# Filling all eight input buffers at the start, and issuing nine later loads from GpSimd as 120 and 8 rows

## The chip, the cores and the metric

The kernel runs on one core of one Trainium2 chip. The metric is the device time of one execution in microseconds (us), the median over the runs named. A profile shows one execution, and its span is the time from the first to the last instruction.

## The reference

```python
# q, k: [8, 12, 1024, 64] float32
def reference(q, k):
    return np.einsum('bhid,bhjd->bhij', q, k).astype(np.float32)   # [8, 12, 1024, 1024]
```

For each of 96 heads a 1024 x 1024 score matrix is written, 4 MB in float32. The profile counts 50.33 MB read from HBM and 402.65 MB written, so outputs are eight ninths of all bytes.

## The kernel before

Heads come in 25 blocks, the first two of two heads, the others of four. A block's input comes in four pieces (two of q, two of k), each 512 KB in blocks of four heads, 4 KB in each of 128 rows. The pieces of the first three blocks go into memory that is later an output buffer ("early"), all others into a pool of eight buffers called x_sb. GpSimd casts a piece to float16, PE transposes it, VectorE copies the transposed tiles, PE multiplies, and ScalarE (5 of 8) and VectorE (3 of 8) evict the scores from PSUM into an output buffer. One DMA of 4 MB per head writes that buffer from the SyncE queue. ScalarE's queue issues the later loads.

```python
    in_pool  = ctx.enter_context(tc.tile_pool(name="in_pool", bufs=8))
    out_pool = ctx.enter_context(tc.tile_pool(name="out_pool", bufs=4))
    # ...
        def load(self, n, eng, raw=None):
            if raw is None:
                x_sb = in_pool.tile([P, self.elems], F32, tag="x")
                raw = x_sb
            self.raw[n] = raw
            start = (self.first + n // 2 * self.G) * S
            src = (qf, kf)[n % 2][start : start + self.G * S]
            pin(eng.dma_start(out=raw, in_=src.rearrange("(p r) d -> p (r d)", p=P)))
    # ... scores(): 8 x (two matmuls of 512 columns, one eviction), then
            pin(nc.sync.dma_start(out=of[self.first + n].rearrange("(p t) j -> p (t j)", p=P),
                                  in_=o_sb.rearrange("p t j -> p (t j)")))
    # ... start: blocks 0 to 2 into "early", then block 3 into four of the eight x_sb
    for n in range(4):
        blocks[3].load(n, (nc.sync, nc.scalar)[n % 2])
    # ... main loop, after each head's scores:
            b.scores(n, side)
            if i == n == 0:
                next_load()          # blocks[4:], piece by piece, nc.scalar
            next_load()
            if nxt and a == nxt.G - 1 and 0 < i + 3 < len(blocks):
                to_half(blocks[i + 3 : i + 4])      # the casts
```

## Time and profile before

The first three runs gave 1074.59 us (1074.47 to 1074.97). Runs of the same kernel fell into two groups, about 1074.3 to 1075.2 and about 1075.8 to 1076.5. The profiled execution was of the second group. What divides the groups was not studied; differences under 1.5 us below rest on several runs, not on one profile.

| what | before |
|---|---|
| time, median | 1074.59 us |
| DMA rate in the middle slices | 426 to 436 GB/s |
| busiest compute engine | PE, 69% of the span |
| first output issued | 19.56 us |

Two views need a word. In the costliest groups a line reads: source line, engine, operation, output<-input, shapes, count, then busy us and mean ns of one, then the idle time just before them and what ended most of it. In the list of DMA issues a line ends with the KB of each and the median us from issue to landing. From these two views of the kernel before:

```profile
L132 ACT COPY o_sb<-ps 128x1024 f32<-128x1024 f32 x480 | 475.9, 1013 | 554.7 <-DMA out_dram<-o_sb 347.6
...
out_dram<-o_sb SPq DMA_DIRECT2D x96, 4096.0 KB, 36.7
```

ScalarE stands idle longer than it works, and most of that waits for an output buffer to be written out. A 4 MB output needs 36.7 us, though 4 MB at 430 GB/s are 9.8 us, because three or four of them stand in the queue at once. The kernel is bound by its DMA engines.

A third reading is not printed on the page. A DMA that all sixteen engines share ends with sixteen increments of its semaphore, one per engine, and the trace records the time of each. Their spread tells how far one engine runs behind the others. I call the time from the fifteenth to the sixteenth increment **the gap**.

### The profile page before, as it was taken

The numbers are of one execution on the slowest core, as the hardware profiler recorded it, in microseconds if no ns is written. First come the engines' busy times: TensorE is split into PE (matmuls) and PEld (weight loads), VectorE is DVE, ScalarE is ACT, GpSimd is POOL, SyncE is SP. The second block draws the span as 40 slices with busy tenths as digits, with TensorE's granted clock in tenths as the row PEclk, the third lists the DMA queues.
The fourth block names the chain that finished last, engine by engine and source line by source line (L and its number), as shares of the span: only waits on it lengthen the run. The fifth ranks groups of instructions, "written<-read, shape, count | busy, mean of one in ns | idle before, by whom it ended". The sixth has DMA issues, their size and how long they took to land.

```text
span 1074.4 us, 6393 instructions
## 1 busy us (share of the span) xinstructions
PE 743.6 (69%) x2304; PEld 267.3 (25%) x2304; DVE 463.7 (43%) x384; ACT 477.2 (44%) x481; POOL 100.7 (9%) x106
## 2 busy tenths in 40 slices
PE   7977677676776757667676676767767676678740
PEld 2322222222222212222222222222222222223210
DVE  4645354452534535345353443434434444445420
ACT  4545444444444434444443544444444443544530
POOL 4100101010010100101010010100101010000000
PEclk9965555555555555555555555555555555555555
DMA  9999999999999999999999999999999999999993
GB/s 332 430 429 433 429 433 432 428 431 433 429 432 431 431 427 436 429 428 435 431 429 434 427 431 434 427 432 434 426 433 433 429 430 432 432 431 429 436 432 170
DMA packets 28257, 453.42 MB, mean 422 GB/s; under 512 B 3136, under 2 KB 3136, under 8 KB 15936
## 3 DMA queue, kind: packets, MB, share of 16 engines
q1 hardware_dynamic: 14976, 405.81, 87.7%
q10 hardware_dynamic: 13248, 47.19, 11.0%
q8 instruction: 18, 0.29, 0.1%
q14 instruction: 15, 0.12, 0.0%
HBM read 50.33 MB, written 402.65 MB: 422 GB/s over the span
## 4 chain that ended last, share of the span: by engine, by line
DMA 79%; PE 12%; ACT 4%; issue 0%; DVE 0%; ACTq 0%; POOL 0%; SPq 0%
DMA out_dram<-o_sb 79%; PE ps L128 12%; ACT o_sb L132 4%; PE t_ps L103 1%; DMA early<-in_q_dram 0%; DVE o_sb L130 0%; DVE kT L115 0%; ACTq L132 0%; POOL half_sb L88 0%; SPq L75 0%
## 5 line engine op out<-in xcount | busy, mean ns | idle before, releaser
L128 PE MATMUL ps<-kT,qT 64*128 64x512 f16 x1536 | 657.3, 621 | 289.8 <-ACT o_sb L132 286.4
L132 ACT COPY o_sb<-ps 128x1024 f32<-128x1024 f32 x480 | 475.9, 1013 | 554.7 <-DMA out_dram<-o_sb 347.6
L130 DVE COPY o_sb<-ps 128x1024 f32<-128x1024 f32 x288 | 352.7, 1225 | 568.9 <-DMA out_dram<-o_sb 404.5
L128 PEld LDWEIGHTS <-qT 64*128 64x128 f16 x1536 | 193.2, 134 | 687.0 <-issue 680.2
L88 POOL CAST half_sb<-x_sb 128x1024 f16<-128x1024 f32 x88 | 91.3, 1040 | 835.0 <-DMA x_sb<-in_k_dram 404.6
L103 PE MATMUL t_ps<-ident,half_sb 128*128 128x128 f16 x768 | 99.0, 310 | 6.1 <-POOL half_sb L88 6.1
L103 PEld LDWEIGHTS <-half_sb 128*128 128x128 f16 x768 | 74.1, 141 | 84.4 <-issue 62.4
L115 DVE COPY qT<-t_ps 128x1024 f16<-128x1024 f16 x48 | 60.6, 1263 | 7.2 <-PE t_ps L103 7.2
L115 DVE COPY kT<-t_ps 128x1024 f16<-128x1024 f16 x48 | 58.3, 1215 | 0.2 <-PE t_ps L103 0.2
L88 POOL CAST half_sb<-early 128x512 f16<-128x512 f32 (+1 forms) x12 | 8.7, 755 | 5.4 <-DMA early<-in_q_dram 5.4
L132 ACT ACT_TABLE_LOAD x1 | 1.3, 1283 | 8.8 <-DMA early<-in_q_dram 8.8
masks.py:199 POOL TENSOR_SCALAR_AFFINE_SELECT ident<-ident 128x128 f16<-128x128 f16 x1 | 0.3, 292 | 0.1
masks.py:197 POOL MEMSET ident<- 128x128 f16 x1 | 0.2, 204 | 0.3 <-POOLq L219 0.3
L219 POOL MEMSET const-float32-0.0<- 128x1 f32 x1 | 0.1, 98 | 0.2 <-issue 0.2
L219 POOL MEMSET const-bfloat16-1.0<- 128x1 bf16 x1 | 0.1, 101 | 0.0
L219 POOL MEMSET const-uint8-127<- 128x1 uint8 x1 | 0.1, 101 | 0.0
L219 POOL MEMSET const-float32-1.0<- 128x1 f32 x1 | 0.1, 98 | 0.0
## 6 DMA issues: line engine op xcount, KB each, us to landing
out_dram<-o_sb SPq DMA_DIRECT2D x96, 4096.0 KB, 36.7
x_sb<-in_k_dram ACTq DMA_DIRECT2D x44, 512.0 KB, 32.1
x_sb<-in_q_dram ACTq DMA_DIRECT2D x42, 512.0 KB, 32.1
early<-in_k_dram ACTq DMA_DIRECT2D x4, 256.0 KB, 5.0
early<-in_q_dram SPq DMA_DIRECT2D x4, 256.0 KB, 4.8
early<-in_q_dram SPq DMA_DIRECT2D x2, 512.0 KB, 7.3
early<-in_k_dram ACTq DMA_DIRECT2D x2, 512.0 KB, 7.4
x_sb<-in_q_dram SPq DMA_DIRECT2D x2, 512.0 KB, 9.3
```

Source lines behind the costliest of these rows:

```text
L88: nc.gpsimd.tensor_copy(out=self.halves[n % 2][:, :, n // 2], in_=self.raw[n].rearrange("p (r d) -> p r d", d=D),)
L103: pin(nc.tensor.transpose(t_ps[:, t], rows, ident))
L115: pin(nc.vector.tensor_copy(out=dst, in_=src))
L128: pin(nc.tensor.matmul(ps[:, js], qT[cs, g, t], kT[cs, g, js]))
L130: pin(nc.vector.tensor_copy(out=o_sb[:, t], in_=ps))
L132: pin(nc.scalar.copy(out=o_sb[:, t], in_=ps))
L219: nc = _bacc.Bacc("TRN2", target_bir_lowering=False, num_devices=1)
```

## The change

Two things are meant to fill idle DMA time at the two ends. At the start all eight x_sb buffers are loaded (blocks 3 and 4) where four were, so that the engines have work until the first output. In mid-run nine q-pieces are issued by GpSimd in two DMAs of 120 and 8 rows; at eight rows per engine, 120 rows leave one engine of sixteen free, which is meant to help an engine that lags. As eight pieces are loaded at once and one more after each head, the later loads also run two heads further ahead.

```diff
-        def load(self, n, eng, raw=None):
+        def load(self, n, eng, raw=None, parts=((0, P),)):
 ...
-            pin(eng.dma_start(out=raw, in_=src.rearrange("(p r) d -> p (r d)", p=P)))
+            src = src.rearrange("(p r) d -> p (r d)", p=P)
+            for lo, hi in parts:
+                pin(eng.dma_start(out=raw[lo:hi], in_=src[lo:hi]))
 ...
-    for n in range(4):
-        blocks[3].load(n, (nc.sync, nc.scalar)[n % 2])
+    stream = [(b, n) for b in blocks[3:] for n in range(4)]
 ...  # next_load() moves up here and takes the issuing engine and the parts
+    for n in range(8):
+        next_load((nc.sync, nc.scalar)[n % 2])
 ...
             b.scores(n, side)
-            if i == n == 0:
-                next_load()
-            next_load()
-            if nxt and a == nxt.G - 1 and 0 < i + 3 < len(blocks):
+            gp = i % 2 == 0 and n == 1 and i > 2
+            if gp:
+                next_load(nc.gpsimd, parts=((0, 120), (120, P)))
+            if nxt and a == nxt.G - 1 and i + 3 < len(blocks):
                 to_half(blocks[i + 3 : i + 4])
+            if i + n > 0 and not gp:
+                next_load(nc.scalar)
```

More of the change, by code (lines that the diff above doesn't have):

```diff
@@ L157, with next_load @@
         at += 4 * b.elems
-    for n in range(4):
-        blocks[3].load(n, (nc.sync, nc.scalar)[n % 2])
+    stream = [(b, n) for b in blocks[3:] for n in range(4)]
+    def next_load(eng, **kw):
+        if stream:
+            b, n = stream.pop(0)
+            b.load(n, eng, **kw)
+    for n in range(8):
+        next_load((nc.sync, nc.scalar)[n % 2])
     make_identity(nc, ident)
@@ L172 @@
     to_half(blocks[2:3])
-    stream = [(b, n) for b in blocks[4:] for n in range(4)]
-    def next_load():
-        if stream:
-            b, n = stream.pop(0)
-            b.load(n, nc.scalar)
     blocks[0].alloc()
```

## The prediction

> **What bounds the kernel now.** I read the page first: the busy shares, then the forty slices with the DMA row, then the queues and the chain that ended last.
>
> ```profile
> PE 743.6 (69%) x2304; PEld 267.3 (25%) x2304; DVE 463.7 (43%) x384; ACT 477.2 (44%) x481; POOL 100.7 (9%) x106
> ...
> DMA  9999999999999999999999999999999999999993
> GB/s 332 430 429 433 429 433 432 428 431 433 429 432 431 431 427 436 429 428 435 431 429 434 427 431 434 427 432 434 426 433 433 429 430 432 432 431 429 436 432 170
> ...
> q1 hardware_dynamic: 14976, 405.81, 87.7%
> q10 hardware_dynamic: 13248, 47.19, 11.0%
> ...
> DMA 79%; PE 12%; ACT 4%; issue 0%; DVE 0%; ACTq 0%; POOL 0%; SPq 0%
> ```
>
> The sixteen DMA engines are busy in every slice but the last, at 426 to 436 GB/s; no compute engine passes 69%, and 79% of the chain is output DMA. So the bytes bound it, and no byte is removed. What is to be had lies in the first slice (332 GB/s) and the last (170). I therefore asked for the windows of both ends (columns: busy time per engine, then granted clock, DMA share, GB/s).
>
> ```profile
> 16.00:18.00 2.00, 2.00 (x14) 1.04 (x13) 1.52 (x3) 0.75 (x1) 0.34 (x1) 1.00 0.93 371
> 18.00:20.00 2.00, 1.76 (x8) 0.44 (x5) 1.56 (x2) 1.47 (x2) 2.00 (x3) 1.00 0.22 35
> 20.00:22.00 2.00, 1.93 (x6) 0.60 (x5) 0.61 (x1) 1.76 (x3) 1.65 (x2) 1.00 1.05 274
> ...
> 1052.00:1056.00 4.00, 0.00 (x0) 0.00 (x0) 0.00 (x0) 0.00 (x0) 0.00 (x0) 0.50 0.95 410
> 1056.00:1060.00 4.00, 0.00 (x0) 0.00 (x0) 0.00 (x0) 0.00 (x0) 0.00 (x0) 0.50 0.42 180
> 1060.00:1062.00 2.00, 0.00 (x0) 0.00 (x0) 0.00 (x0) 0.00 (x0) 0.00 (x0) 0.50 0.08 33
> 1068.00:1070.00 2.00, 0.00 (x0) 0.00 (x0) 0.00 (x0) 0.00 (x0) 0.00 (x0) 0.50 0.08 33
> ```
>
> The tail is the find. From 1060 to 1072 us the share is about one sixteenth: **one engine of sixteen** is still writing. A transfer's end is sixteen semaphore increments, one per engine, and the trace has the time of each. For the last output the first came at 1056.23, the eighth at 1058.71, the fifteenth at 1060.51 and the sixteenth at 1072.83 us: 12.3 us for one engine alone. The same gap was 0.07 us for the output issued at 75.9, 1.06 at 163.7, 6.06 at 430.9, 8.83 at 697.5 and 11.61 at 875.2. So one engine falls behind evenly, all run long. The packets say how: of the 12288 packets of 32 KB nearly all took 1213 ns, but between 60 and 1045 us 769 took 3 to 90 ns more, 15.6 us in total, and one engine's share of 96 outputs is 96 x 8 = 768. It is slower by some 20 ns a packet (1.7%) and is never idle.
>
> Then the start, from the timeline of the first 25 us.
>
> ```profile
> 7.05 1.70 ACTq L75 DMA_DIRECT2D x_sb<-in_k_dram  x2
> 8.78 1.28 ACT L132 ACT_TABLE_LOAD   x1 [8.78 <-DMA early<-in_q_dram]
> 10.39 1.01 ACT L132 COPY o_sb<-ps 128x1024 f32<-128x1024 f32 x1 [0.33 <-PE ps L128]
> 18.53 1.01 ACT L132 COPY o_sb<-ps 128x1024 f32<-128x1024 f32 x1 [1.77 <-PE ps L128]
> 18.53 0.34 ACTq L75 DMA_DIRECT2D x_sb<-in_q_dram  x1
> 19.56 23.82 SPq L136 DMA_DIRECT2D out_dram<-o_sb  x4
> ```
>
> Inputs run dry at 18.1 us; the packets restart at 19.6 with two loads, slowly (274 GB/s at first), and the first output issues at 19.56. ACT's first copy comes only after its queue has issued its loads, the last of which waited until 8.4 us for an earlier transfer's semaphore.
>
> **What the Trainium skill says.** "DMA: Bandwidth & Descriptors", section "Where 436 GB/s comes from", puts the ceiling at sixteen ports times 27.2 GB/s, 435 GB/s; the slices at 426 to 436 agree, so the middle cannot be sped up. The same page, "Latency and other measured facts", says engines 7 and 15 are usually slower and guesses at the rings of GpSimd-issued DMAs. This trace agrees that one engine is slower, but no GpSimd-issued DMA exists in it, so the guessed cause does not hold here; the trace does not number the engine. The same page, "Why a DMA increments its semaphore by 16 and not by 1", says how many engines a DMA uses: a 128-partition copy takes all sixteen; some GpSimd-issued direct copies are given ceil(partitions/16) rows per engine, so that 100 partitions leave engine 15 without data. No run shows that yet; the change stands on it. "SBUF — State Buffer", section "SBUF: two separate sides", warns that GpSimd cannot write descriptors while a VectorE operation holds the shared port. GpSimd casts of 1040 ns with no spread beside DVE copies (43% busy) show no such lock-out here.
>
> **The change, part by part.**
>
> (a) *Nine of the 88 x_sb loads as 120 + 8 rows from GpSimd.* With 8 rows per engine, 120 rows fill engines 0 to 14 and leave the sixteenth free; 8 rows then go as one row each to eight engines. A 4 KB packet repeats every 155 ns on a busy engine. The sixteenth engine is spared 9 x 8 x 155 = 11.2 us. Eight others get 9 x 155 = 1.4 us more. The pieces are one in two blocks, about 89 us apart by the chain's 44.4 us per block; 1.24 us relieved each time against a growth of 12.3 us / 1000 us x 89 = 1.1 us: the sizes match so well that I take the sixteenth engine to be the target. Issuing costs nothing on the path: POOL is 9% busy, and its DMAs stand in its order behind casts that are long done.
>
> (b) *Four more loads at the start.* They are 2 MB, 4 x 8 x 155 = 5.0 us of every engine, so data lasts to 18.1 + 5.0 = 23.1 us instead of 18.1. But two more go through ACT's queue, and the instruction order of the changed kernel shows them ahead of the table load, each waiting for a reused semaphore: by the trace of before, those early transfers land at 11.11 and 13.67 us. ACT then loads its table at about 14.1 and first copies at 15.4 instead of 10.39. PE has three output banks and stalls on the fourth tile. Walking copies of 1.01 (ACT) and 1.22 us (DVE) and matmul pairs of 0.9 us forward in their order, I get the first output at 22.9 instead of 19.56 us. So the hole is not filled outright: loads end at 23.1 and the output's packets begin 1 to 3.7 us after issue (3.7 is what the first one of before took, 23.3 - 19.56). Loss before: 1.6 us empty plus about 1.4 us of slowed load packets (23 us excess over 16 engines). Loss after: 0.8 to 3.5 us. Net gain some 0.8 us, between -0.5 and +2. Later outputs (29.6, 38.3 us) come before the engines have drained.
>
> (c) *Loads running two heads further ahead.* The queue was never empty; worth nothing.
>
> Sum: the slow engine ends at 1072.8 - 0.8 - 11.2 = 1060.8; the fifteenth, with added rows, at 1060.5 - 0.8 + 1.4 = 1061.1. With 1.6 us from last landing to the end of the span (1074.4 - 1072.8), that is 1062.7 us. Both ends meet, so no further gain hides behind it.
>
> **The rivals.** *First: the relieved engine is another one.* Nothing numbers the slow engine. If it is among those that take the extra 8 rows, it ends 1.4 us later, some 1075 us; if the engine left out changes from one DMA to the next, the relief is spread and the slow one gets nothing net, some 1074. For it: the page's two candidates, 7 and 15. Against: the fit of nine pieces to the lag, in size and spacing. I give these together 30%. *Second: the start gets worse*, by ACT's blocked queue, as worked out in (b): up to 1.5 us against the gain. That is included. *Third: GpSimd's DMAs are costly themselves*, by slow descriptor writing or by slowing an engine whose ports hold the rings. A late piece is covered by about five heads (55 us) from issue to cast; eighteen such DMAs against 184 others can hardly slow an engine by more than 1 to 3 us. That would give 1063 to 1066. *Fourth: the slow engine had held back the others*, so that more than the tail comes back. The fifteen were busy throughout, so there is no more to give.
>
> **Range and chances.** About 65% for 1060.5 to 1064.5, about 30% for 1072.5 to 1075.5, the rest between or outside. The point leans on the first, with a little for the third rival: 1063.5. Over 2% faster means under 1053.1. The engines' own load of 96 x 8 x 1.2095 + 88 x 8 x 0.155 + about 10 us of early loads = 1048 us, the first bytes at 1.75 us, some 3 us lost before the first output, 196 semaphore writes of 9 ns (1.8), the added rows (1.4) and the end (1.6) already come to 1057.5: 2%. Slower by over 2% needs 21 us more, which no step offers: 2%.
>
> **What would show it.** Right: one-sixteenth windows after the other engines end shrink from 12 us to under 3; the gap of sixteenth to fifteenth increment stays below 3 us all run instead of growing to 12; the GpSimd-issued loads carry 120- and 8-row packets with the main queues' 4 KB packets fewer by 9 x 128; ACT's table load near 14 us, first output at 22 to 24. Wrong: the gap again grows to 11 to 14 us (another engine relieved); table load still at 8.8 (my reading of the queue fails); DMA share under 0.9 in a middle slice (a new wait).

## The result

Four runs of the changed kernel gave a median of 1075.04 us (1074.91 to 1075.21), beside 1074.78 us for four of the kernel before. The ratio is 1.000, with a 95% interval of 0.9983 to 1.0017. (A ratio here is the mean time of one kernel's runs over that of the other's of the same rounds, so it is not quite the ratio of the medians quoted.) Nothing was gained.

The page of the changed kernel, in the same rows as before: the DMA row and the GB/s of the forty slices, the queues (packets, MB, share of sixteen engines' span) and the chain.

```profile
DMA  9999999999999999999999999999999999999993
GB/s 391 425 425 433 426 432 430 421 434 429 433 420 434 434 424 431 433 429 430 430 429 428 431 432 428 430 434 427 435 432 422 434 435 427 431 431 438 430 430 171
...
q1 hardware_dynamic: 15264, 406.85, 88.2%
q10 hardware_dynamic: 11664, 41.42, 9.5%
q0 software_dynamic: 1584, 4.72, 1.1%
...
DMA 77%; PE 12%; ACT 4%; issue 0%; ACTq 0%; SPq 0%
```

The first slice rose from 332 to 391 GB/s, so the start did improve. The last slice is 171 where it was 170: the tail is as it was. The new row q0 is GpSimd's nine pieces, 4.72 MB. Its 1584 packets are 1152 of 4096 bytes, the nine times 128 rows, and 432 of four bytes.

The windows of the start (columns: busy time and count of PE, PE's weight loads, VectorE, ScalarE and GpSimd, then granted clock, DMA share, GB/s):

```profile
16.00:18.00 2.00, 2.00 (x5) 0.58 (x5) 0.96 (x1) 1.82 (x3) 0.00 (x0) 1.00 1.04 416
18.00:20.00 2.00, 2.00 (x12) 0.91 (x12) 1.39 (x2) 0.96 (x1) 0.07 (x1) 1.00 1.01 403
20.00:22.00 2.00, 1.76 (x7) 0.55 (x4) 1.56 (x3) 1.20 (x2) 2.00 (x3) 1.00 1.04 416
22.00:24.00 2.00, 2.00 (x5) 0.53 (x4) 0.89 (x1) 1.82 (x3) 1.93 (x2) 1.00 1.28 533
```

No window is empty any more. From 16 to 22 us the kernel before moved 371, 35 and 274 GB/s and this one 416, 403 and 416. The differences sum to 555 GB/s over 2 us, 1.1 MB, which is some 2.6 us at 430 GB/s (an estimate from these windows). The 533 GB/s from 22 to 24 us is no true rate: a window counts a packet whole where it starts, and the first 32 KB packets start here. The timeline of ScalarE shows the delay that the prediction walked through:

```profile
6.94 6.67 ACTq L77 DMA_DIRECT2D x_sb<-in_k_dram  x4
13.64 1.28 ACT L134 ACT_TABLE_LOAD   x1 [13.64 <-DMA early<-in_k_dram]
14.93 2.84 ACT L134 COPY o_sb<-ps 128x1024 f32<-128x1024 f32 x3
```

The table load did move behind the four issues, from 8.78 to 13.64 us, and the first copy to 14.93. The first output was issued at 21.84 us.

The windows of the tail, the same columns:

```profile
1058.00:1060.00 2.00, 0.00 (x0) 0.00 (x0) 0.00 (x0) 0.00 (x0) 0.00 (x0) 0.50 0.15 66
1060.00:1062.00 2.00, 0.00 (x0) 0.00 (x0) 0.00 (x0) 0.00 (x0) 0.00 (x0) 0.50 0.04 16
...
1068.00:1070.00 2.00, 0.00 (x0) 0.00 (x0) 0.00 (x0) 0.00 (x0) 0.00 (x0) 0.50 0.04 16
1070.00:1072.00 2.00, 0.00 (x0) 0.00 (x0) 0.00 (x0) 0.00 (x0) 0.00 (x0) 0.50 0.04 16
```

One engine of sixteen still writes alone, for over ten microseconds. The last output's increments came at 1052.84 (first), 1055.95 (8th), 1060.50 (15th) and 1071.88 us (16th). The gap is 11.4 us where it was 12.3. In the kernel before, the first and the eighth came at 1056.23 and 1058.71, about three microseconds later: some engines did end earlier, but not the one that sets the end.

**Which engine carries what.** The packets in the trace do not name their engine, but on a busy engine each packet starts 3 to 4 ns before the last one ends, so a chain of packets can be followed. In the stretches around the GpSimd pieces this yields sixteen chains: one with no 4 KB packet of the piece, seven with eight, eight with nine. That is the arithmetic of the prediction: 120 rows on fifteen engines, the 8 further rows on eight. The slow engine can be told by its 32 KB packets, which take some 21 ns longer in the median. In every piece that could be read (for instance 470 to 492 and 740 to 757 us) it carried **nine**. The change gave the lagging engine one row more, not eight fewer. Where packets of two engines end together, their chains can be mistaken for each other; the increments, read under gp128 below, do not have this weakness and say the same.

### The profile page after: what moved, and what is told of

The parts are those of the page before. It is cut to its first block, busy times and chain, and to the rows that moved or that the text cites. A ratio compares the mean times of both kernels' runs of the same rounds, so it can differ in the third digit from the quotient of the medians.

```text
span 1073.1 us, 6371 instructions
## 1 busy us (share of the span) xinstructions
PE 744.3 (69%) x2304; PEld 267.6 (25%) x2304; DVE 463.7 (43%) x384; ACT 476.9 (44%) x481; POOL 106.8 (10%) x124
## 3 DMA queue, kind: packets, MB, share of 16 engines
q0 software_dynamic: 1584, 4.72, 1.1%
## 4 chain that ended last, share of the span: by engine, by line
DMA 77%; PE 12%; ACT 4%; issue 0%; ACTq 0%; SPq 0%
DMA out_dram<-o_sb 71%; PE ps L130 11%; DMA x_sb<-in_q_dram 6%; ACT o_sb L134 4%; PE t_ps L105 0%; ACTq L134 0%; SPq L138 0%
## 5 line engine op out<-in xcount | busy, mean ns | idle before, releaser
L90 POOL CAST half_sb<-x_sb 128x1024 f16<-128x1024 f32 x88 | 88.4, 1044 | 801.7 <-PE t_ps L105 414.4
L77 POOL DMA_DIRECT2D x_sb<-in_q_dram x18 | 9.5, 532 | 0.0
```

The lines of the kernel that those rows point to most:

```text
L77: pin(eng.dma_start(out=raw[lo:hi], in_=src[lo:hi]))
L90: nc.gpsimd.tensor_copy(out=self.halves[n % 2][:, :, n // 2], in_=self.raw[n].rearrange("p (r d) -> p r d", d=D),)
```

## The experiments

All edits are to the changed kernel, unless it is said otherwise. The kernel before ran beside each call.

### start_only, gp128, gp_only: the parts alone

```diff
 # start_only: every later load from ScalarE, as before
-            gp = i % 2 == 0 and n == 1 and i > 2
+            gp = False
 # gp128: GpSimd issues the same nine pieces, each as one DMA of 128 rows
-                next_load(nc.gpsimd, parts=((0, 120), (120, P)))
+                next_load(nc.gpsimd)
 # gp_only: the kernel before, with the nine pieces from GpSimd as 120 + 8 rows
+            if i % 2 == 0 and n == 1 and i > 2:
+                next_load(nc.gpsimd, parts=((0, 120), (120, P)))
+            else:
+                next_load()
```

> The start of the change alone: eight x_sb buffers filled at the beginning, every later load from ACT as 128 rows, no GpSimd DMA. Theory (the two parts cancel: the start gains about 2 us, the uneven pieces cost the slow engine 9 rows x 155 ns = 1.4 us): 2.0 to 2.5 us faster than before, ratio 0.9977 to 0.9982. Rival 1 (the start gains nothing, as ACT's late table load eats it): within 0.5 us of before. Rival 2 (GpSimd DMAs cost as such): says nothing of this run. The gap between fifteenth and last increment of the last output stays at 11 to 13 us in all.

> The changed kernel, but the nine GpSimd loads are one DMA of 128 rows each. Theory (only the extra row on the slow engine costs): as start_only within 0.5 us, so 1.4 us faster than the changed kernel. Rival 2 (a GpSimd DMA costs whatever its shape, by descriptors or ring traffic): as the changed kernel or slower, near 1075. In the trace every engine should carry 8 data packets of each piece.

> The kernel before with nine of its later loads issued by GpSimd as 120 and 8 rows, its start untouched. Theory (slow engine gets 9 rows instead of 8 of each piece): 1.4 us slower than before, ratio 1.001 to 1.002, gap of the last increment 12 to 14 us. Rival (the spared engine is the slow one after all, and something else ate the gain): 8 to 11 us faster, gap under 4 us.

Measured, five rounds each, with 1074.79 us for the kernel before:

| kernel | median us | ratio to before (95%) |
|---|---|---|
| start_only | 1072.63 | 0.9979 (0.9967 to 0.9992) |
| gp128 | 1073.55 | 0.9989 (0.9976 to 1.0001) |
| gp_only | 1076.68 | 1.0018 (1.0004 to 1.0032) |

The start alone gains 2.2 us. Handing nine whole pieces to GpSimd gives back 0.9 us (1073.55 - 1072.63, with ranges that do not touch: 1072.29 to 1073.00 and 1073.26 to 1074.02). Cutting each into 120 + 8 gives back 1.5 us more (1075.04 - 1073.55; after_again, on the same chip as gp128, gives 1.6). Nine pieces, each with one 155 ns row and one 9 ns semaphore write more for the slow engine, come to 9 x 0.164 = 1.48 us. The sum -2.2 + 0.9 + 1.5 = +0.2 gives back the measured 0.3, as it must, since the three are steps from one kernel to the next; what supports it from outside is the 1.48. On the start of before, the second part alone makes the kernel slower, by 1.9 us, where 0.9 + 1.5 would be 2.4.

Two expected gaps were missed: gp_only's is 11.3 us (12 to 14 expected), and start_only's 4.6 us (11 to 13), with the fifteenth increment at 1064.50, the sixteenth at 1069.07 and the other fourteen by 1061.68. So in that execution two engines lag, and the gap alone understates the lag. The gap of gp128's last output is 11.0 us against 11.4 with the cut. By the increments of the slow engine, eight outputs around a piece take 88.87 us in gp128 and 89.03 in the changed kernel, a difference of 0.16 per piece: the ninth row is seen piece by piece.

### locate: which cuts hit the slow engine

Each of the nine pieces was cut in another way, to see from the slow engine's increments where the rows fall.

```diff
+    # ... cut(): the rows as ranges of these sizes
+    shapes = [cut(120, 8), cut(120, 4, 4), cut(120, 2, 2, 2, 2), cut(120, 3, 3, 2),
+              cut(120, 5, 3), cut(120, 6, 2), cut(120, 7, 1), cut(*[8] * 16), cut(P)]
-                next_load(nc.gpsimd, parts=((0, 120), (120, P)))
+                next_load(nc.gpsimd, parts=shapes.pop(0) if stream else ())
```

> Look only: the changed kernel with nine different cuts of the GpSimd pieces: 120 rows and then 8; 4+4; 2+2+2+2; 3+3+2; 5+3; 6+2; 7+1; then sixteen DMAs of 8; then one of 128. If a DMA of n < 16 rows puts one row on each of the n lowest engines, the slow engine (the one whose 32 KB packets take some 20 ns more) carries 9 rows of the first piece, and the others tell its number: 10 or 8 (4+4), 12 or 8 (2+2+2+2), and so on; 16 rows of the piece of sixteen DMAs if it is among the lower eight, 0 if not. Rival (a moving first engine): its counts follow no such pattern. The time should grow by the extra rows, 8 x 155 ns = 1.2 us for the sixteen-DMA piece, and at most 1.5 us for the rest.

1076.75 us, not a time to compare. The clear mark is the eighth piece: sixteen DMAs of 8 rows cost the slow engine 1.56 us more than the whole piece at the same place in gp128, about what eight extra rows (8 x 0.155 = 1.24) and further semaphore writes make. So the slow engine is among those that take one of 8 rows. The remainders cut as 5 + 3, 6 + 2 and 7 + 1 moved it by 0.28, 0.15 and 0.23 us, those as 3 + 3 + 2 and four times 2 by 0.07 and 0.12. These fit an engine that takes a row of a 5-row DMA and not of a 4-row one, which would be the fifth, but differences of 0.1 us are too near the scatter to rest on.

### hw120: the same cut from ScalarE's queue

```diff
-                next_load(nc.gpsimd, parts=((0, 120), (120, P)))
+                next_load(nc.scalar, parts=((0, 120), (120, P)))
```

> The changed kernel, but its nine uneven pieces (120 and 8 rows) are issued by ACT instead of GpSimd. Theory (start gain 2.2 us; GpSimd issue as such costs 0.9 us, the uneven cut 1.5 us by the slow engine's ninth row): 2.2 - 1.5 = 0.5 to 1.0 us faster than before, ratio about 0.9993. Rival (the cost is all GpSimd's): as start_only, 0.998. Rival (ACT's cut spares the slow engine): 8 us faster or more.

A miss: 1077.55 us against 1074.92, ratio 1.0019 (1.0007 to 1.0032). The GB/s row of its page shows something else than the question asked:

```profile
GB/s 388 423 425 435 423 415 429 427 433 433 425 432 434 427 429 435 427 427 437 427 428 428 424 433 423 424 433 421 394 429 431 391 419 427 434 432 431 429 430 286
```

Two slices in the middle fall to 394 and 391 GB/s: the DMA engines ran short there. The fifteenth increment of the last output came at 1067.31 and the sixteenth at 1073.23 us, so the gap shrank to 5.9 us because the other engines had become late too. The extra issues in ScalarE's queue wait for earlier landings, and the copies behind them wait along; I did not prove that this is the cause. The run says nothing about what a row or a GpSimd issue costs. That stays open.

### lower_half: nine pieces, each as sixteen DMAs of 8 rows

If the slow engine is among the eight that always take the 8 rows, it now gets sixteen rows a piece instead of eight.

```diff
-                next_load(nc.gpsimd, parts=((0, 120), (120, P)))
+                next_load(nc.gpsimd, parts=[(r, r + 8) for r in range(0, P, 8)])
```

> The changed kernel with each of the nine GpSimd pieces cut into sixteen DMAs of 8 rows, so that eight engines take 16 rows each and eight none. Theory (the slow engine is one of those eight): 9 x 7 rows x 155 ns = 9.8 us more than the changed kernel and some 2 to 3 us for the many semaphore writes, 1086 to 1089 us, gap of the last increment over 15 us. Rival (the slow engine is the one that 120 rows spare, or any of the upper eight): it loses 9 x 8 rows, 11 us, and the time is 1064 to 1068.

Measured 1088.08 us, ratio 1.0118 (1.0104 to 1.0132), as expected under the theory that the slow engine is one of those eight. The windows of its tail:

```profile
1066.00:1068.00 2.00, 0.00 (x0) 0.00 (x0) 0.00 (x0) 0.00 (x0) 0.00 (x0) 0.50 0.46 197
...
1070.00:1072.00 2.00, 0.00 (x0) 0.00 (x0) 0.00 (x0) 0.00 (x0) 0.00 (x0) 0.50 0.57 246
...
1082.00:1084.00 2.00, 0.00 (x0) 0.00 (x0) 0.00 (x0) 0.00 (x0) 0.00 (x0) 0.50 0.08 33
```

About half of the engines work from 1066 to 1072 us: those are the eight with the doubled rows (the 8th increment came at 1065.94, the 15th at 1077.68). Then one remains, to 1085.07. The slow engine is in the loaded half. The gap is 7.4 us, not over 15 as expected, because the fifteenth engine is then one of the seven others with doubled rows; from the eighth increment to the last it is 19.1 us.

### extra_mm: more PE instructions, no more data

What makes that engine slow? In the kernel before, the delay of slow 32 KB packets grows, though not at every step, with the number of matmuls and transposes that start while the packet is under way (the 769 packets delayed by 3 to 90 ns between 60 and 1045 us; a few of them are of other engines):

```
PE instructions in the packet's time     0      1      2      3      4      5      6      7
mean delay of a slow packet, ns        9.5   13.1   21.4   19.4   28.8   30.1   28.6   40.1
```

The last compute instruction ends at 1040.7 us, and the slow engine's packets at the end, from 1062.7 us on, are not delayed: each takes 1213 ns. So I added 1536 tiny matmuls, whose results the next matmul overwrites, to start_only.

```diff
 # on top of start_only
                     js = slice(j * 512, (j + 1) * 512)
+                    tiny = slice(j * 512, j * 512 + 16)
+                    pin(nc.tensor.matmul(ps[:, tiny], qT[cs, g, t], kT[cs, g, tiny]))
                     pin(nc.tensor.matmul(ps[:, js], qT[cs, g, t], kT[cs, g, js]))
```

> start_only with a matmul of 16 columns ahead of each of the 1536 score matmuls (overwritten by it; the result stays right). It asks what slows the slow engine. In the trace its delay per 32 KB packet goes with the number of PE instructions in it, some 3 to 4 ns each. Theory (instruction traffic of the core slows that engine): 1536 more matmuls and weight loads add 4 to 9 us to its lag, gap 15 to 21 us, time 4 to 8 us over start_only, with the other fifteen engines ending where they did. Rival (the delay is the engine's own): time within 0.7 us of start_only, 1072.6, gap 11 to 13 us.

Measured 1080.27 us, ratio 1.0046 (1.0032 to 1.0059), 7.6 us over the median of start_only (from another call). Not a byte of input or output was added. The slow engine's last increment came at 1077.03 where it had been 1069.07 us (8.0 later), the eighth at 1061.61 where it had been 1058.73 (2.9 later). That the others would stay as they were was wrong by 2.9 us, but the slow engine lost over twice as much. By its increments, four outputs take it 44.36 us in start_only and 44.72 in extra_mm, which is 11 ns for each of 32 packets. The expected gap of 15 to 21 us was missed (10.6, against 4.6 in start_only), since the fifteenth increment is late too, at 1066.41, 4.8 us after the eighth. The first outputs were issued at the same time in both (22.01 and 21.89 us), so the start is not the cause. The instruction fetches, from the pages of start_only and of extra_mm, did grow:

```profile
q8 instruction: 18, 0.29, 0.1%
```

```profile
q8 instruction: 30, 0.49, 0.2%
```

Twelve more fetches of 16 KB, each about 0.94 us of one engine, are 11 us, or 0.7 us if spread over sixteen. Where chains of packets could be followed, in the kernel before and in extra_mm, the fetches ran on other engines than the slowest, and that engine's own 32 KB packets were the ones prolonged. So the fetched bytes do not explain its lag. What is shown is that the lag grows when PE has more instructions; through which path is not shown. One rival was not tested: the profiler records every instruction, and every run has a span and a clock, so the traffic of that recording may itself be what delays the engine.

### locate2: other access patterns

```diff
+    shapes = [ ...  # 120 and 8 rows as column halves, as two 1 KB chunks per row ("3d"),
+               ...  # 100 + 28 rows, 60 + 60 + 8 rows, 127 rows "3d" + 1 row, 128 rows "3d" ]
-                next_load(nc.gpsimd, parts=((0, 120), (120, P)))
+                next_load(nc.gpsimd, parts=shapes.pop(0) if stream else ())
```

> Look only: other forms of the nine pieces (halves of columns, three-dimensional patterns, 100+28 rows, 60+60+8, 127+1), to see whether any of them places its rows on other engines than the lowest. If they all fill from the lowest engine, the slow engine never carries fewer rows than an even cut gives it, and 11 us cannot be had this way. If some start at a moving engine, the engine without rows differs from piece to piece.

1083.31 us, useless as a time: the piece of 127 rows in two chunks went to a single engine, landed only at 899.7 us, 159 us after it was issued, and left the other engines short of work at its end (one slice fell to 207 GB/s). What it was worth running for: with rows in two chunks, a half-piece of 120 rows left out a *different* engine each time. Two engines then carried four to five rows of a piece, the others nine. This is the other rule that the Trainium skill states in "DMA: Bandwidth & Descriptors", section "Why a DMA increments its semaphore by 16 and not by 1": the count of engines is the largest number up to 16 that divides the rows, and for GpSimd's DMAs with fewer than sixteen engines they are consecutive ones "from a round-robin cursor". The plain rows tried here filled from the lowest engine, so what they leave out are the last engines, and they do not lighten one in the lower half. The moving form can, if it is aimed.

### sweep and spare34: find the engine, and spare it

126 rows divide by 14, so two engines are left out of a half-piece and the cursor moves on by 14. sweep lets it run; spare34 first sets it with a 5-row DMA, and then each of nine pieces is cut so that the cursor returns and the *fourth and fifth* engines are left out every time.

```diff
 # sweep
-                next_load(nc.gpsimd, parts=((0, 120), (120, P)))
+                next_load(nc.gpsimd, parts=[(0, 126, 0), (0, 126, 1), (126, P, "rows")])
 # spare34 (0 and 1: the half-piece of two chunks; 3: that half as two plain DMAs)
 ...  # load() takes this third entry; in sweep too
+    def shift(by):
+        return [(0, by, 0), (0, by, 3), (by, P, "rows")]
+    aimed = [(0, 126, 0), (126, P, 0), (0, 126, 1), (126, P, 1)]
+    shapes = [shift(5)] + 9 * [aimed] + [shift(11)]
-            gp = i % 2 == 0 and n == 1 and i > 2
+            gp = n == 1 and (i % 2 == 0 and i > 2 or i in (3, 19))
+                next_load(nc.gpsimd, parts=shapes.pop(0) if stream else ())
```

> Look only: nine pieces in column halves of 126 rows each, with the last 2 rows plain, so that the two engines left out move on by two with every half. If a moving start exists, the slow engine is left out in one half of eighteen in every eight halves, in the same piece and its fourth successor: pieces 3 and 7 if it is the third or fourth engine from the start, 2 and 6 (counted from 0) if the fifth to eighth... that is, its rows of that piece fall from 9 to about 4 or 5. If no start moves, it carries 9 rows in each piece or none.

> An attempt at what the change meant to do. In the looks before, plain DMAs of fewer than 16 rows filled from the lowest engine, and the slow engine's counts put it at the fourth or fifth; three-dimensional ones (two chunks of 1 KB per row) spared a different engine each time, as if each began where the last one ended. Nine pieces go as column halves of 126 rows (9 rows on each of 14 engines) and 2 rows (one on each of the two left out), which brings the start back to where it was; a first piece of 5 rows moves the start by five, so that the fourth and fifth engine are the two left out; a last piece of 11 rows moves it on to a full round. If the start is at the first engine when the kernel begins and the number is right: the slow engine carries 1 row instead of 8 of nine pieces, 9 x 7 x 155 ns = 9.8 us less, the other fourteen 1.4 us more, 1062 to 1066 us, gap under 4 us. Rival (the start or the number is another): the slow engine carries 9 rows, 1075 to 1079 us, gap 11 us or more, and the two engines spared end early.

In sweep (one look, 1074.39 us) four outputs with a piece among them take the slow engine 44.7 us, but 44.03 and 44.05 us in the third and the seventh piece. A half-piece is nine half-rows per engine, 9 x 0.155 / 2 = 0.7 us, so there it was left out once. By the cursor's steps these two pieces are the ones that leave out the fifth to eighth engines. With spare34 the only engine in both sets is the **fifth** (number 4, counted from 0 in the cursor's order). This takes the cursor to stand at the first engine when the kernel starts, which no run shows by itself; the 5 + 3 cut of locate, which does not use the cursor, points to the same engine.

spare34 measured 1069.29 us (1069.12 to 1069.79) against 1076.24 for the kernel before, which fell mostly in its upper group. The ratio is 0.9938 (0.9924 to 0.9951). It beats both kernels. The windows of its tail:

```profile
1056.00:1058.00 2.00, 0.00 (x0) 0.00 (x0) 0.00 (x0) 0.00 (x0) 0.00 (x0) 0.50 0.91 393
1058.00:1060.00 2.00, 0.00 (x0) 0.00 (x0) 0.00 (x0) 0.00 (x0) 0.00 (x0) 0.50 0.38 164
...
1064.00:1066.00 2.00, 0.00 (x0) 0.00 (x0) 0.00 (x0) 0.00 (x0) 0.00 (x0) 0.50 0.04 16
1066.00:1068.00 2.00, 0.00 (x0) 0.00 (x0) 0.00 (x0) 0.00 (x0) 0.00 (x0) 0.50 0.01 4
```

The sixteen engines stay together longer (393 GB/s from 1056 to 1058 us, 213 in the changed kernel), and the lone stretch after 1062 us is some four microseconds long. The gap is 1.4 us for the output landing at 811 us, 4.2 at the end: it grows back after the last piece. Whether the last engine is then still the fifth, or a second slow one as in start_only, was not followed. The size was still missed: I had expected 1062 to 1066. The others paid for it: the eighth increment came at 1059.35 us against 1056.10 in gp128. Their ninth row explains 1.4 of those 3.2 us; the rest was not taken apart.

### misaim and after_again: the control

misaim issues the same number of DMAs of the same kinds as spare34, but with the cursor set so that the fifteenth and sixteenth engines are left out. after_again is the changed kernel once more on the same chip.

```diff
 # misaim, on top of spare34
-    shapes = [shift(5)] + 9 * [aimed] + [shift(11)]
+    shapes = [shift(16)] + 9 * [aimed] + [shift(16)]
```

> Control for spare34: the same DMAs in the same form, but the first and last piece shift the start by sixteen instead of five and eleven, so that the nine pieces leave out the fifteenth and sixteenth engine. Theory (it is the aim that gains): the slow engine carries 9 rows of each of the nine pieces, 72 x 155 ns = 11 us more than in spare34 at most, though there other engines end some 4 us earlier than it; 1075 to 1078 us, gap 10 to 13 us. Rival (the form gains, not the aim): as spare34, 1069 us, gap about 4 us.

> The changed kernel once more, beside the kernel before and misaim on one chip, for the sum of the parts: start 2.2 us faster, GpSimd issue 0.9 us and the ninth row 1.4 us slower: within 0.6 us of before, ratio 0.999 to 1.001. In the trace the slow engine carries 9 rows of every piece, as on the first chip.

misaim: 1076.32 us, ratio 1.0009 (0.9996 to 1.0021). after_again: 1075.12 us, ratio 0.9997 (0.9983 to 1.0011), beside 1075.17 us. The tail of misaim:

```profile
1060.00:1062.00 2.00, 0.00 (x0) 0.00 (x0) 0.00 (x0) 0.00 (x0) 0.00 (x0) 0.50 0.27 115
1062.00:1064.00 2.00, 0.00 (x0) 0.00 (x0) 0.00 (x0) 0.00 (x0) 0.00 (x0) 0.50 0.04 16
...
1070.00:1072.00 2.00, 0.00 (x0) 0.00 (x0) 0.00 (x0) 0.00 (x0) 0.00 (x0) 0.50 0.08 33
```

The lone stretch is back, to 1073.34 us where spare34's last increment came at 1066.05, with a gap of 9.8. The same DMAs aimed at other engines gain nothing, so what spare34 gains is the aim. The two ran on different chips (1 and 9), but they are 7.0 us apart, and the kernels before beside them only 1.1; that the slow engine has the same number on every chip was not tested. The changed kernel is the same mistake in its plain form: it relieves the sixteenth engine, which has time to spare.

## Why the prediction was wrong

**What bounds the kernel: right.** DMA holds 77% of the chain and the middle slices stay at 420 to 438 GB/s.

**The tail as one lagging engine: right.** It is still there, it is shorter where the aim was right (spare34), and it grows with load put on that engine (lower_half). (The gaps of start_only and hw120 are shorter too, 4.6 and 5.9 us, but because a second engine or all others were late.) Start_only's profile showed two slow engines instead of one; how many there are in an execution was not studied further. One supporting count was luck: 769 slowed packets beside one engine's 768 looks like proof of a single engine, but the counted stretch holds 11679 packets of 32 KB, some 730 of each engine, so at least 39 of the 769 belong to others.

**Step (a) failed**, at "the sizes match so well that I take the sixteenth engine to be the target". The rows were placed as worked out, and the sixteenth engine was spared. But the slow engine is another one, by sweep and spare34 the fifth, and in place of the 11.2 us it was to be spared it took 9 x 0.155 us more. Three runs show this independently: nine rows in its chain of packets, lower_half's 13 us, and spare34 against misaim. The fit of nine pieces to the lag, in size and spacing, was a coincidence as far as the trace can tell. It was an argument about what somebody may have intended with the change, and no view of the profile stood behind it. The first rival named the true course ("it ends 1.4 us later, some 1075 us") and got 30%, together with the moving left-out engine. The step could have been settled without a run only if the trace had numbered its engines, and it does not. So the chances should have leaned the other way: by counting alone, of the slow engine's sixteen possible places one is spared, eight get a row more, and seven stay as they are.

**Step (b): the mechanism right, the size off.** Table load at 13.64 (14.1 predicted), first copy 14.93 (15.4), first output 21.84 us (22.9). The term that was mis-sized is "Loss after: 0.8 to 3.5 us". It was nothing: loads lasted to 23.2 us (23.1 predicted), the output came 1.1 us sooner than walked, and its packets began at 22.73, some 0.9 us after the issue, not up to 3.7. The engines did not run dry in between, and the start gained 2.2 us by start_only, where I had said 0.8.

**Step (c), loads running further ahead:** nothing contradicts its worth of zero, but no run tried it alone.

**"Issuing costs nothing on the path": off by 0.9 us**, the difference of gp128 and start_only. The third rival had allowed 1 to 3. GpSimd spends 9.5 us in all on eighteen issues:

```profile
L77 POOL DMA_DIRECT2D x_sb<-in_q_dram x18 | 9.5, 532 | 0.0
L134 ACT ACT_TABLE_LOAD x1 | 1.3, 1283 | 13.6 <-DMA early<-in_k_dram 13.6
```

That time stands beside idle time of GpSimd and is not the cost. In gp128 the number of packets under 512 bytes is 3136, as in the kernel before, so it is not extra semaphore writes either. Where the 0.9 us comes from stays open.

**The sum also mixed two clocks.** It ended at a span of 1062.7 us, and I gave that as a time. A time is 1.8 us longer than its span, which the single profile and the median hid because the profiled execution was one of the kernel's longer ones. Corrected, the forecast is 1064.5 us, still over ten microseconds below the measured 1075.04.

## What to carry to other kernels

When one engine of a set lags, a change that moves load must be shown to move it off *that* engine: follow its packets, or run the same transfers aimed at another engine as a control, before a match of sizes is believed. Where DMA binds, read the sixteen increments of an output's semaphore and not only the bytes per second; a slice row at full speed hides an engine that falls 1% behind. And measure the parts of a change alone: here a gain of 2.2 us at the start was hidden by two losses of 0.9 and 1.5 us.

## What the Trainium skill lacked or had wrong

- "DMA: Bandwidth & Descriptors", section "Latency and other measured facts", calls engines 7 and 15 usually slower, and guesses at the rings of GpSimd's DMAs. Here the slow one is the fifth (number 4 in the cursor's order), in a kernel without one GpSimd DMA: 12.3 us behind at the end.
- "SBUF — State Buffer", section "SBUF: two separate sides", says that "A DMA cannot be slowed by a compute op". Of the memory's ports that may hold; but 1536 tiny matmuls without a byte of data delayed the slow engine by 8.0 us and the kernel by 7.6. No page was found that has one DMA engine lag with the core's instructions. Whether the engine's work or its recording by the profiler does it is open.
- The first page's section "Where 436 GB/s comes from" holds: the middle slices are at 420 to 438 GB/s here. Its remark that HBM, at about 358 GB/s, binds transfers between HBM and SBUF does not hold for this kernel, which runs on one core: it moved 422 GB/s over its whole span. The 358 is, by the same remark, half of what two cores share.
- The first page's section "Why a DMA increments its semaphore by 16 and not by 1" says that "some" direct copies of GpSimd are given by ceil(rows/16). Here those of plain rows were (fifteen engines with eight of 120 rows), and those of rows in two chunks went by the divisor and the cursor. It says that all sixteen engines post an increment, but not that an engine without a row handles one more four-byte packet in that row's place: nine pieces cut in two gave 432 such packets, of which 18 x 16 = 288 are increments; nine whole ones gave 144, all increments.
- Beyond first-byte latencies, no page was found with what a plain load from GpSimd costs a kernel that DMA binds, beside one from ScalarE's queue: nine of 512 KB cost 0.9 us here.
